# Queries and probabilities moved through DRAM with one write each, and the query split pinned behind the key copies, in a two-layer attention encoder

## The chip, the cores and the metric

The kernel runs on one core of a Trainium2 chip. The metric is the device time of one execution in microseconds. The median of three runs before the change is 906.31 us (905.59 to 910.03).

## The reference, cut to what matters

```python
D_MODEL = 1024; SEQ = 512; DEPTH = 2; HEAD_DIM = 64; N_HEADS = 16
DILATED_PAIRS = ((128, 1), (512, 4), (2048, 16))

def reference(x, norm_gain, a_w_in, a_w_out, ..., b_rpb):
    for i in range(DEPTH):
        hn = rms_norm(x, norm_gain[i])
        y = mixer_a(hn, ...) if i % 2 == 0 else mixer_b(hn, ...)
        x = x + y

def mixer_a(hn, w_in, w_out, q_gain, k_gain, t5_bias):
    proj = hn @ w_in                   # 3 groups of q, k, v, and one gate
    for g, (window, dilation) in enumerate(DILATED_PAIRS):
        q = rms_norm(qkv[:, :, g, 0], q_gain[g]); k = rms_norm(qkv[:, :, g, 1], k_gain[g])
        o, lse = dilated_group_attention(q, k, v, t5_bias[...], dilation, reach)
    alpha = softmax(stack(lses)); y = sum(alpha * stack(outs))
    return (y * silu(gate)) @ w_out
```

The first layer is a dilated sliding-window attention in three dilation groups, merged by their softmax denominators. The second (`mixer_b`) is a neighbourhood attention on an 8 x 64 grid with one group of q, k, v and a gate. All is float32.

## The kernel before, in words

Heads are worked in eight pairs (`hc` = 0 to 7, 128 columns each). A float32 product is made of three matmuls of split operands (`mm3`: high x high, high x low, low x high). Weights come in loads of 128 x 1024 (`wraw`, three buffers, L175), are split on ScalarE (`wh`, L127) and on VectorE or GpSimd (`wl`, L131), and are used by TensorE as `acc` matmuls, 128x512 each.

Two generators are run side by side. `main` emits the projections of a pair: keys and values of groups 1 and 2 (`rawk`), the queries and the keys of group 0 (`rawq`), the values of group 0 (`vt`), the gate (`gt`). `side` emits the attention of the pair before. `run` weaves them by a clock that counts matmul time, and `later_on(delay, job)` puts a job into the order at a due time of that clock, in ns. TensorE's order is the order written; on the other engines a scheduler of the framework places instructions by its own model, except those given to `tc.keep_in_program_order`. All transfers but two small ones are issued by SyncE (SP) in one queue. A transfer's issue also waits for the completion of the one eight places ahead of it, since eight completion counters are used in turn.

For one pair of the first layer the steps around the change are these.

- The projected keys and values are copied from PSUM to `rawk` on ScalarE (L458, eight copies of 128x256). GpSimd squares the keys (L272), VectorE reduces them, GpSimd computes the scale factors `rs` (L108 to L120), VectorE scales the keys (L295).
- `turn_q` transposes the scaled queries in 32x32 blocks on VectorE, in place in `rawq`. For pairs 0 to 5 (`moved`) `move_q` then sends them with sixteen SBUF-to-SBUF transfers of 64 KB into `qt` (L578), which completes the transposition.
- `split_q` makes the split operands of the group-0 scores: `k0h` (ScalarE, L598), `q0h` (ScalarE, L617 in `put_k`), `k0l` and `q0l` (VectorE, L601, L619). It is emitted after the key projection of the next pair, and is not pinned.
- The weighted sum of the earlier pair (`o` matmuls) is multiplied into its gate (`gt`, L668), which frees its PSUM bank. The scores (`log` matmuls) take four banks of the same pool of four, in two halves, u = 0 and 1.
- VectorE adds the bias and finds the extreme (`p`, L786, L797), ScalarE does the exponential (L808) and scaling (L648), VectorE transposes blocks into `tr` (L720). `turner.send` writes `tr` to DRAM (`td`, L729) in four writes of 256 KB, and reads it back into `pt` in four reads (L733), each into 32 partitions.
- The bias tiles `e` are loaded by six transfers for each pair (L683, L688).

In the second layer the probabilities of pairs 0 to 5 are moved by the same `turner.send`, with 224 KB for each write and read.

Of the kernel before, what the change touches and what calls it, by code (L numbers as in the profile page):

```python
# [13 lines left out]
F32 = mybir.dt.float32  # L14
F32R = mybir.dt.float32r
I32 = mybir.dt.int32
AF = mybir.ActivationFunctionType
# [5 lines left out]
P = 128  # L23
# [19 lines left out]
def tile_hybrid_encoder(  # L43
# [13 lines left out]
    nc = tc.nc  # L57
# [8 lines left out]
    dr = ctx.enter_context(tc.tile_pool(name="dr", bufs=1, space=DRAM))  # L66
# [132 lines left out]
    stamp = {(key, -1): 0 for key in ("k12", "q", "v", "qk")}  # L199
# [26 lines left out]
    def later_on(delay, job):  # L226

        timers.append((clock[0] + delay, job))
        timers.sort(key=lambda t: t[0])
# [132 lines left out]
    gk = cp.tile([P, 4], F32, name="gk")  # L362
# [55 lines left out]
    pq = wk.tile([P, 4096], F32, tag="pt", name="pt", bufs=1)  # L418
# [51 lines left out]
    def normed(raw, ss, ns, key, hc):  # L470
        head_norm(raw, ss, ns, key == "raw")
        if key == "rawq" and moved(hc):
            turn_q(raw)
        st[key, hc] = raw
        stamp[key, hc] = clock[0]
# [53 lines left out]

    def turn_q(raw):  # L530

        for a in range(0, 16, 4):
            v = raw[:, a : a + 4].rearrange("p f i r -> p (f i) r")
            nc.vector.transpose(v, v)

    def q_tiles():


        return (
            wk.tile([P, 512], F32R, tag="q0h", name="q0h", bufs=1),  # L540
            wk.tile([P, 512], F32R, tag="q0l", name="q0l", bufs=1),
            wk.tile([P, 4, 4, P], F32, tag="q12", name="qt", bufs=1),
            wk.tile([P, EXT], F32R, tag="k0h", name="k0h", bufs=1),
            wk.tile([P, EXT], F32R, tag="k0l", name="k0l", bufs=1),
        )
# [22 lines left out]

    def move_q(hc, raw):

        tiles = q_tiles()
        qt, left = tiles[2], [4]

        def move(a):
            for t in range(4):
                src = raw[32 * t : 32 * t + 32, 4 * a : 4 * a + 4].rearrange("k f i r -> k (f i r)")
                dst = qt[32 * a : 32 * a + 32, t].rearrange("k f x -> k (f x)")
                tc.keep_in_program_order(nc.sync.dma_start(dst, src))  # L578
            left[0] -= 1
            if a == 3:  # L580
                stamp["q", hc] = 0

        for a in range(4):
            later_on(1400 * a, partial(move, a))

        def land():
            yield "wait", ("rawk", hc + 1), 0
            assert not left[0]
            split_q(*tiles)
            st["q", hc] = tiles  # L590
            yield

        st["land", hc] = land()

    def split_q(q0h, q0l, qt, k0h, k0l):
        src = qt[:, :, 3, :].rearrange("p t (j r) -> p t r j", j=4)
        trj4 = lambda t: t[:, 64:EXT].rearrange("p (t r j) -> p t r j", t=4, j=4)
        nc.scalar.copy(trj4(k0h), src)  # L598
        by_t = lambda t: t.rearrange("p (t x) -> p t x", t=4)
        put_k([(by_t(q0h), by_t(q0l), qt[:, :, 0, :])], 0)  # L600
        nc.vector.tensor_sub(trj4(k0l), src, trj4(k0h.bitcast(F32)))  # L601

    def v_a(hc):

        yield "wait", ("vt", hc), 2500
        vt = st.pop(("vt", hc))
        tp = bank("tp")
        for i in range(4):
            transpose(tp[:, i * P : (i + 1) * P], vt[:, i * P : (i + 1) * P])
        nc.scalar.copy(v0[hc % 2], tp.rearrange("p (i c) -> p i c", i=4))  # L610
        stamp["v", hc] = 0
        yield

    def put_k(parts, g):

        for dh, _, src in parts:
            nc.scalar.activation(dh, src, AF.Copy, scale=gk[:, g : g + 1])  # L617
        for dh, dl, src in parts:
            nc.vector.scalar_tensor_tensor(  # L619
                dl, src, gk[:, g : g + 1], dh.bitcast(F32), op0=ALU.mult, op1=ALU.subtract  # L620
            )
# [87 lines left out]
    class turner:  # L709
# [12 lines left out]
        def send(self, dst, wait, pace):  # L722

            run = self.run
            d = dr.tile([4, P, run], F32, tag="td", name="td", bufs=2)
            place = dst.rearrange("p (a x) -> p a x", a=4)

            def write(b):
                tc.keep_in_program_order(nc.sync.dma_start(d[b], self.t[:, b * run : b * run + run]))  # L729

            def read(b):
                src = d[b].rearrange("(a k) x -> k a x", a=4)
                tc.keep_in_program_order(nc.sync.dma_start(place[32 * b : 32 * b + 32], src))  # L733
                self.left -= 1

            for b in range(4):
                later_on(pace * b, partial(write, b))
                later_on(wait + pace * b, partial(read, b))

    def attn_a(hc):  # L740
        e0, e12 = st.pop(("e", hc))
        q0h, q0l, qt, k0h, k0l = st.pop(("q", hc))
# [5 lines left out]
        def scores(u):  # L748

            tiles = []  # L750
            for t in (2 * u, 2 * u + 1):
                cs, n = (64, 192) if t == 0 else (0, 192) if t == 3 else (0, 256)
                tiles.append((t, [bank("log") for _ in range(2)], cs, n))
            for t, lgs, cs, n in tiles:
                ks = slice(P * t + cs, P * t + cs + n)
                qs = slice(P * t, P * t + P)
                mm3_heads(
                    [lg[:, cs : cs + n] for lg in lgs],
                    lambda hs: q0h[hs, qs], lambda hs: q0l[hs, qs],
                    lambda hs: k0h[hs, ks], lambda hs: k0l[hs, ks], False,  # L760
                )
            for t, lgs, cs, n in tiles:
                for g in range(2):
                    for j in range(4):
                        for hd in range(2):
                            hs = slice(64 * hd, 64 * hd + 64)
                            matmul(
                                lgs[hd][32 * j : 32 * j + 32, 256 + P * g : 384 + P * g],
                                qt[hs, t, 1 + g, 32 * j : 32 * j + 32],
                                k12[hs, g, P * j : P * j + P],  # L770
                                share=2,
                                start=False,
                                stop=(g == 1),
                            )
            return [
                (hd, t, softmax(hd, t, lgs[hd], cs, n)) for t, lgs, cs, n in tiles for hd in range(2)
            ]
# [34 lines left out]
        def turn_p(hd, t, pr):  # L812
            tp = bank("tp")
            for i in range(4):
                transpose(tp[:, i * P : (i + 1) * P], pr[:, i * P : (i + 1) * P])
            dst = sb(pts[0], at(t, 0, hd, 0), [[32, 4], [512, 4], [1, 32]])
            nc.vector.tensor_copy(dst, tp.rearrange("p (i a r) -> p i a r", i=4, a=4))
# [25 lines left out]
        if hc < NHC - 1:  # L843
            for u in range(2):
                if moved(hc):
                    if pending and u == 0:
                        pending.pop(0)()
                        yield
                    yield "wait", ("rawk", hc + 1), 4800 if u == 0 else 18500
                else:  # L850
                    yield 1200 if u == 0 else 8500
                turned = turner(512)
                turners.append(turned)
                for hd, t, pr in scores(u):
                    turned.put(pr, 512, 256 * hd + 128 * (t % 2))
                send = partial(turned.send, pq[:, 2048 * u : 2048 * u + 2048], 10500 - 1000 * u, 1200)
                later_on(7000 + 2000 * u, send)
                if pending and u == 0:
                    yield 5000
                    pending.pop(0)()  # L860
            pending.append(lambda: put_y(hc, weigh(), True, False))
        else:
            for u in range(2):
                if u == 0:
                    yield "wait", ("gate", hc), 500
                yield 600
                held = scores(u)
                yield 3200
                if pending:
                    yield "wait", ("gate", hc - 1), 16800  # L870
                    pending.pop(0)()
                    yield
                for args in held:
                    turn_p(*args)
                    yield
            yield from v_a(hc)
            stamp["ya", "turned"] = 0
            put_y(hc, weigh(), True, True)
            yield
# [392 lines left out]
```

## Time and profile before

| | |
|---|---|
| median of 3 runs | 906.31 us (905.59 to 910.03) |
| profiled execution, its own time | 905.46 us |
| its span | 903.7 us |
| TensorE busy, matmuls | 856.8 us (95%), 5547 |
| VectorE, ScalarE, GpSimd busy | 524.4, 427.6, 305.6 us |
| DMA | 134.97 MB, mean 149 GB/s |
| mean granted TensorE clock | 0.979 |

How to read the rows that follow. A row of the order of time gives the start and duration in us, the engine (PE is TensorE, DVE VectorE, ACT ScalarE, POOL GpSimd, SPq the queue of transfers on SyncE), the line of the kernel, the operation, output and inputs, a count, and in brackets the idle time before it with what ended it. A row of waits gives who waited for whom, the total in us, the number of times, and the longest. A row of the chain gives start, duration and what. A row of windows gives the stretch, its length, the busy time of TensorE's matmuls and weight loads, VectorE, ScalarE and GpSimd with counts, then the granted clock, the DMA engines' busy share and GB/s.

### The profile page before, as it was taken

What the parts mean: (1) busy time and instruction counts of PE and PEld (TensorE: products, weight loads), DVE (VectorE), ACT (ScalarE), POOL (GpSimd) and SP (SyncE); (2) the same over time, 40 slices, a digit from 0 to 9 for tenths busy, and PEclk for the clock granted to TensorE, in tenths of its full rate; (3) what the DMA queues carried; (4) which work ended last, traced back from release to release, by engine and by line L of the source; (5) the groups of instructions that cost most, each with busy time, mean ns of one, the idle gap of its engine ahead of it and who ended that gap; (6) DMA issues with size and microseconds to landing.
All of it is one profiled execution on the core that took longest, in us unless ns stands there. A gap on an engine that the chain in (4) does not pass through costs nothing.

```text
span 903.7 us, 15576 instructions
## 1 busy us (share of the span) xinstructions
PE 856.8 (95%) x5547; PEld 708.5 (78%) x5547; DVE 524.4 (58%) x1335; ACT 427.6 (47%) x924; POOL 305.6 (34%) x493
## 2 busy tenths in 40 slices
PE   8999999898799699699789999999999999999998
PEld 6788877687588488578668878778999888899776
DVE  6354594483576268258267675546566667666743
ACT  6434554452552363345255355445465556665541
POOL 2342532351442324234144134111433454434411
PEclk9999999999899899799989999999999999999999
DMA  6354287357257437634726847236326555656233
GB/s 235 105 147 128 91 244 188 108 143 209 84 162 211 126 109 204 162 118 114 215 78 170 235 130 198 66 121 219 99 87 180 161 150 150 165 157 178 101 102 126
DMA packets 64318, 134.97 MB, mean 149 GB/s; under 512 B 7920, under 2 KB 25264, under 8 KB 64240
## 3 DMA queue, kind: packets, MB, share of 16 engines
q1 hardware_dynamic: 63952, 133.96, 51.6%
q8 instruction: 44, 0.72, 0.3%
q14 instruction: 34, 0.28, 0.1%
q10 hardware_dynamic: 288, 0.01, 0.0%
HBM read 102.82 MB, written 24.83 MB: 141 GB/s over the span
## 4 chain that ended last, share of the span: by engine, by line
PE 67%; DMA 17%; DVE 5%; ACT 4%; SPq 4%; issue 2%; POOL 1%; ACTq 0%; DVEq 0%; POOLq 0%
PE acc L206 55%; DMA wraw<-in_w 7%; DMA td<-tr 5%; PE log L206 5%; PE o L206 4%; DMA e<-l_d 3%; SPq L578 2%; PE tp L210 2%; DMA qt<-rawq 1%; DVE wl L131 1%; DVE p L797 1%; ACT p L808 1%; ACT rawk L458 1%; ACT wh L127 1%; DMA pt<-td 1%
## 5 line engine op out<-in xcount | busy, mean ns | idle before, releaser
L206 PE MATMUL acc<-wh,hn_h 128*128 128x512 f32 (+1 forms) x768 | 299.0, 389 | 36.5 <-ACT rawk L458 34.6
L127 ACT CAST wh<-wraw 128x512 fp32r<-128x512 f32 (+1 forms) x276 | 161.1, 588 | 319.0 <-PE acc L206 217.2
L206 PE MATMUL acc<-wl,hn_h 128*128 128x512 f32 (+1 forms) x768 | 289.5, 377 | 0.4 <-DVE wl L131 0.4
L206 PE MATMUL acc<-wh,hn_l 128*128 128x512 f32 (+1 forms) x768 | 289.7, 377 | 0.0
L131 POOL TENSOR_TENSOR wl<-wraw,wh 128x512 fp32r<-128x512 f32 (+1 forms) x110 | 140.5, 1277 | 407.3 <-ACT wh L127 372.6
L206 PEld LDWEIGHTS acc<-wh,hn_h 128*128 128x128 f32 x768 | 146.8, 191 | 67.8 <-ACT rawk L458 37.1
L131 DVE TENSOR_TENSOR wl<-wraw,wh 128x512 fp32r<-128x512 f32 (+1 forms) x166 | 121.6, 733 | 134.5 <-ACT wh L127 129.7
L206 PEld LDWEIGHTS acc<-wh,hn_l 128*128 128x128 f32 x768 | 146.6, 191 | 21.6
L206 PEld LDWEIGHTS acc<-wl,hn_h 128*128 128x128 f32 x768 | 147.1, 192 | 20.1 <-DVE wl L131 0.9
L206 PE MATMUL acc<-hn_h,wh 128*128 128x512 f32 x192 | 77.8, 405 | 1.0 <-ACT rawq L458 0.8
L206 PE MATMUL acc<-hn_l,wh 128*128 128x512 f32 x192 | 75.0, 391 | 0.0
L206 PE MATMUL acc<-hn_h,wl 128*128 128x512 f32 x192 | 75.0, 391 | 0.0
L272 POOL TENSOR_TENSOR sq<-rawk 128x256 f32<-128x256 f32 x64 | 42.5, 676 | 87.2 <-ACT rawk L458 80.5
L648 ACT ACTIVATE p<-p,mn 128x512 f32<-128x512 f32 (+3 forms) x128 | 68.6, 586 | 0.0
L808 ACT ACTIVATE p<-p,mn 128x512 f32<-128x512 f32 (+1 forms) x64 | 44.9, 702 | 48.7 <-DVE mn L797 48.7
L720 DVE STREAM_TRANSPOSE tr<-p 128x512 f32<-128x512 f32 (+1 forms) x80 | 53.6, 683 | 9.4 <-ACT p L648 9.0
L273 DVE TENSOR_REDUCE ss<-sq 128x4 f32<-128x256 f32 (+1 forms) x96 | 48.1, 502 | 18.5 <-POOL sq L272 15.1
L206 PE MATMUL acc<-y_h,wh 128*128 128x512 f32 x128 | 52.1, 407 | 0.0
L206 PE MATMUL acc<-y_h,wl 128*128 128x512 f32 x128 | 50.0, 391 | 0.0
L206 PE MATMUL acc<-y_l,wh 128*128 128x512 f32 x128 | 50.0, 390 | 0.0
L206 PEld LDWEIGHTS acc<-hn_h,wh 128*128 128x128 f32 x192 | 36.1, 188 | 12.7 <-ACT rawq L458 2.9
L206 PEld LDWEIGHTS acc<-hn_h,wl 128*128 128x128 f32 x192 | 36.0, 188 | 7.9
(138 smaller groups left out, 1072.3 us busy)
## 6 DMA issues: line engine op xcount, KB each, us to landing
wraw<-in_w SPq DMA_DIRECT2D x95, 512.0 KB
wraw<-in_w SPq DMA_DIRECT2D x38, 384.0 KB
td<-tr SPq DMA_DIRECT2D x56, 256.0 KB
pt<-td SPq DMA_DIRECT2D x56, 256.0 KB
qt<-rawq SPq DMA_DIRECT2D x96, 64.0 KB
td<-tr SPq DMA_DIRECT2D x24, 224.0 KB
pt<-td SPq DMA_DIRECT2D x24, 224.0 KB
e<-l_d SPq DMA_DIRECT2D x32, 112.0 KB
```

Source lines behind the costliest of these rows:

```text
L127: nc.scalar.copy(h, raw)
L131: eng.tensor_sub(l, raw, h.bitcast(F32))
L206: nc.tensor.matmul(o, l, r, **kw)
L210: nc.tensor.transpose(o, i, ident)
L272: nc.gpsimd.tensor_mul(sq, v, v)
L273: nc.vector.tensor_reduce(ss[:, i * ns : (i + 1) * ns], sq.rearrange("p (a b) -> p a b", b=64), axis=AX.X, op=ALU.add)
L458: nc.scalar.activation(dst, src, AF.Copy, scale=rs_n[:, i : i + 1])
L578: tc.keep_in_program_order(nc.sync.dma_start(dst, src))
L648: nc.scalar.activation(pr, pr, AF.Copy, scale=mn[:, 3:4])
L720: nc.vector.transpose(dst, src[:, :n].rearrange("p (i b k) -> p i b k", b=4, k=32))
L797: nc.vector.tensor_tensor_reduce(out=v(pr), in0=v(lg), in1=e12[:, 2 * hd : 2 * hd + 2, 96 - 32 * t : 224 - 32 * t], scale=1.0, scalar=mn[: ...
L808: nc.scalar.activation(row, row, AF.Exp, bias=mn[:, 1:2], scale=-1.0, accum_out=mn[:, 2:3])
```

## The change

The queries go to a DRAM tile with one write of 1 MB and come back in four reads of 256 KB, in the order 0, 2, 1, 3. The write is due 600 ns after the start of `move_q`, the reads 5500 ns after it. The probabilities are written in one transfer too; their reads stay four, in the same changed order. The two copies of the query split on ScalarE are kept in program order, behind the key copies of the next pair. `turn_q` runs its four transposes over the token blocks. Three due times of the scores and of the sends are moved: 4800 to 5200, 18500 to 17800, and the wait of the reads from 10500 and 9500 to 8500.

```diff
     def turn_q(raw):
-        for a in range(0, 16, 4):
-            v = raw[:, a : a + 4].rearrange("p f i r -> p (f i) r")
-            nc.vector.transpose(v, v)
+        for i in range(4):
+            nc.vector.transpose(raw[:, :, i, :], raw[:, :, i, :])
...
     def move_q(hc, raw):
+        d = dr.tile([4, P, 512], F32, name="qd", tag="qd", bufs=2)
         tiles = q_tiles()
         qt, left = tiles[2], [4]
-        def move(a):
-            for t in range(4):
-                src = raw[32 * t : 32 * t + 32, 4 * a : 4 * a + 4].rearrange("k f i r -> k (f i r)")
-                dst = qt[32 * a : 32 * a + 32, t].rearrange("k f x -> k (f x)")
-                tc.keep_in_program_order(nc.sync.dma_start(dst, src))
+        def write():
+            src = raw.rearrange("p (a f) i r -> p a (f i r)", f=4)
+            tc.keep_in_program_order(nc.sync.dma_start(d.rearrange("a p x -> p a x"), src))
+            stamp["q", hc] = 0
+        def read(a):
+            dst = qt[32 * a : 32 * a + 32].rearrange("k t f x -> k t (f x)")
+            src = d[a].rearrange("(t k) x -> k t x", t=4)
+            tc.keep_in_program_order(nc.sync.dma_start(dst, src))
             left[0] -= 1
-            if a == 3:
-                stamp["q", hc] = 0
-        for a in range(4):
-            later_on(1400 * a, partial(move, a))
+        later_on(600, write)
+        for a in (0, 2, 1, 3):
+            later_on(5500, partial(read, a))
...
     def split_q(q0h, q0l, qt, k0h, k0l):
-        nc.scalar.copy(trj4(k0h), src)
+        tc.keep_in_program_order(nc.scalar.copy(trj4(k0h), src))
-        put_k([(by_t(q0h), by_t(q0l), qt[:, :, 0, :])], 0)
+        put_k([(by_t(q0h), by_t(q0l), qt[:, :, 0, :])], 0, True)
...
-    def put_k(parts, g):
+    def put_k(parts, g, pinned=False):
         for dh, _, src in parts:
-            nc.scalar.activation(dh, src, AF.Copy, scale=gk[:, g : g + 1])
+            m = nc.scalar.activation(dh, src, AF.Copy, scale=gk[:, g : g + 1])
+            if pinned:
+                tc.keep_in_program_order(m)
...
     class turner: def send(self, dst, wait, pace):
-            def write(b):
-                tc.keep_in_program_order(nc.sync.dma_start(d[b], self.t[:, b * run : b * run + run]))
+            src = self.t[:, : 4 * run].rearrange("p (b x) -> p b x", b=4)
+            tc.keep_in_program_order(nc.sync.dma_start(d.rearrange("b p x -> p b x"), src))
-            for b in range(4):
-                later_on(pace * b, partial(write, b))
-                later_on(wait + pace * b, partial(read, b))
+            for n, b in enumerate((0, 2, 1, 3)):
+                later_on(wait + pace * n, partial(read, b))
...
     def attn_a(hc):
-                    yield "wait", ("rawk", hc + 1), 4800 if u == 0 else 18500
+                    yield "wait", ("rawk", hc + 1), 5200 if u == 0 else 17800
-                send = partial(turned.send, pq[:, 2048 * u : 2048 * u + 2048], 10500 - 1000 * u, 1200)
+                send = partial(turned.send, pq[:, 2048 * u : 2048 * u + 2048], 8500, 1200)
```

## The prediction

> **What bounds the kernel now.** I read the page first, then who waited for whom on TensorE, then TensorE's order of time for its longer gaps.
>
> ```profile
> span 903.7 us, 15576 instructions
> PE 856.8 (95%) x5547; PEld 708.5 (78%) x5547; DVE 524.4 (58%) x1335; ACT 427.6 (47%) x924; POOL 305.6 (34%) x493
> ```
> ```profile
> PE acc L206 <- ACT rawk L458: 34.6, 5, 8.5
> PE log L206 <- DVE gt L668: 2.4, 1, 2.4
> ...
> PE acc L206 <- DVE wl L131: 0.4, 1, 0.4
> ```
> ```profile
> 154.34 0.50 PE L206 MATMUL acc<-wh,hn_h 128*128 128x512 f32 x1 [1.74 <-ACT rawk L458]
> ...
> 165.03 0.38 PE L206 MATMUL log<-k0h,q0h 64*128 64x256 f32 x1 [2.40 <-DVE gt L668]
> ...
> 231.74 0.79 PE L206 MATMUL acc<-wh,hn_h 128*128 128x512 f32 x1 [8.37 <-ACT rawk L458]
> ...
> 305.97 0.79 PE L206 MATMUL acc<-wh,hn_h 128*128 128x512 f32 x1 [7.96 <-ACT rawk L458]
> ...
> 380.31 0.80 PE L206 MATMUL acc<-wh,hn_h 128*128 128x512 f32 x1 [7.95 <-ACT rawk L458]
> ...
> 455.77 0.79 PE L206 MATMUL acc<-wh,hn_h 128*128 128x512 f32 x1 [8.55 <-ACT rawk L458]
> ```
>
> TensorE is busy for 856.8 of 903.7 us, so nearly all that can be won without removing matmuls is its 46.9 us of idle time. Most of it is six gaps, all in the first layer: four of about 8 us, one for each of head pairs 2 to 5, and two small ones around pair 1. In the large ones TensorE has finished the next pair's keys and wants their accumulators back; ScalarE has not copied them out (L458). ScalarE's and SyncE's orders of time, and the chain that ended last, tell why:
>
> ```profile
> 303.50 1.06 ACT L598 CAST k0h<-qt 128x512 fp32r<-128x512 f32 x1 [6.47 <-DMA qt<-rawq]
> ...
> 305.10 3.01 ACT L458 ACTIVATE rawk<-acc,rs_n 128x256 f32<-128x256 f32 x8
> ```
> ```profile
> 268.38 0.34 SPq L729 DMA_DIRECT2D td<-tr  x1
> 279.68 0.30 SPq L733 DMA_DIRECT2D pt<-td  x1
> ...
> 288.16 13.75 SPq L578 DMA_DIRECT2D qt<-rawq  x16
> ```
> ```profile
> 231.74 3.66 PE acc L206 x9
> ...
> 240.62 1.99 PE log L206 x75
> ...
> 301.32 2.01 DMA qt<-rawq
> ...
> 305.97 4.05 PE acc L206 x9
> ...
> 317.23 11.80 PE acc L206 x51
> ...
> 380.31 4.21 PE acc L206 x9
> ...
> 455.77 4.21 PE acc L206 x9
> ```
>
> The split of the queries (k0h, L598) stands ahead of the eight key copies on ScalarE and sat 6.47 us waiting for the moved queries. Their sixteen small DMAs took 13.75 us to issue. So a late transfer held work that does not need it. After each gap the clock is low as well: nine matmuls took 3.66 to 4.21 us, where 51 in a row took 11.80, or 0.231 each and 2.08 for nine.
>
> **Part by part. (1) The pin.** In the compiled order of the changed kernel all six pairs have the eight key copies, then one weight cast, then the query split. The four large waits go: 8.37 + 7.96 + 7.95 + 8.55 = 32.8 us. Their slow restarts go too: 3.66 + 4.05 + 4.21 + 4.21 = 16.1 less 4 x 2.08, which is 7.8. Pair 1 offers its two gaps and the half clock after the second:
>
> ```profile
> 154.40:156.60 2.20, 2.20 (x9) 1.40 (x9) 1.83 (x4) 2.20 (x7) 2.05 (x4) 1.00 0.00 0
> 165.10:169.70 4.60, 4.60 (x76) 3.50 (x77) 3.36 (x19) 3.29 (x7) 1.53 (x1) 0.64 0.00 0
> ```
>
> These are windows; the third column from the right is the granted clock. The gap of 1.74 us left it at 1.00, the one of 2.40 was followed by 0.64 for 4.6 us, a loss of 4.6 x 0.36 = 1.7. Pair 1 has 1.74 + 2.40 + 1.7 = 5.8. All that can go is 32.8 + 7.8 + 5.8 = 46.4 us, or 9.3 for each of five pairs.
>
> **(2) What is late next: VectorE.** In the changed order VectorE does the key scaling (L295) ahead of the product that frees the output's PSUM bank (gt, L668). Before, only pair 1 had that order, and its 2.40 us gap is the price. The rows:
>
> ```profile
> 161.88 2.50 DVE L295 TENSOR_TENSOR rawk<-rawk,rs 128x256 f32<-128x256 f32 x4 [3.95 <-POOL rs L120]
> 164.30 0.67 DVE L668 TENSOR_TENSOR gt<-gt,o 128x512 f32<-128x512 f32 x1
> ```
> ```profile
> 313.31 0.22 POOL L120 TENSOR_TENSOR rs<-rs,na 128x16 f32<-128x16 f32 x1
> ```
> ```profile
> 314.30 1.42 DVE L295 TENSOR_TENSOR rawk<-rawk,rs 128x256 f32<-128x256 f32 x4
> ```
> ```profile
> 162.33 0.30 PE L206 MATMUL log<-k0h,q0h 64*128 64x256 f32 x1
> ```
>
> Let K be the moment TensorE has finished a pair's keys. GpSimd's scale factors were ready 313.53 - 308.11 = 5.4 us after the last copy (305.10 + 3.01). Copies that wait for nothing end a quarter of 3.01 us after K, at K + 0.8, so the factors come at K + 6.2. Scaling is 1.42 or 2.50 and the product 0.67: the bank is free at K + 8.3 to K + 9.4. TensorE wants it 162.33 - 154.34 + 0.2 = 8.2 us after it goes on from K. That leaves a wait of 0.1 to 1.2 us in each of pairs 1 to 5. I take 1.2, the row in which GpSimd works beside VectorE as it will here. Between 1.74 (no half clock) and 2.40 (half clock) lies the threshold; small delays can push 1.2 over it, so I add half of 1.7: 2.0 us a pair, 10 us in all, between 0.5 and 14.5.
>
> The Trainium skill, "TensorE: Matmul & The Clock Gate", section "What's actually happening", puts the fall to half rate after an idle window of about 3.4 us. By that the waits would cost 1.2 a pair, 6 in all, and the time would be 4 us lower. The trace is harsher: a 2.40 us gap was followed by half rate.
>
> **(3) The queries through DRAM.** Nothing in the trace shows this round trip, so it is built from windows. (last column GB/s)
>
> ```profile
> 281.00:293.00 12.00, 12.00 (x56) 9.91 (x56) 3.51 (x7) 4.05 (x8) 2.59 (x2) 1.00 1.01 290
> 296.00:302.00 6.00, 2.02 (x9) 1.32 (x8) 0.69 (x1) 0.62 (x1) 0.00 (x0) 1.00 0.39 90
> 342.00:347.00 5.00, 5.00 (x23) 4.13 (x22) 4.65 (x8) 1.00 (x2) 3.73 (x4) 1.00 1.06 230
> ```
>
> The first is a full queue (290 GB/s), the second the small query copies alone (90), the third mostly the four reads of probabilities (230). Count from the scores' start S = 240.62; K was 305.97 - 7.96 = 298.0, S + 57.4. The second write of probabilities landed by 279.68, S + 39.1; being four times as large it takes about 2 us more, S + 41. In the new order four reads (1 MiB), three weights (1.5 MiB) and the query write (1 MiB) follow: 3.67 MB at 290 GB/s is 12.7 us, S + 54. The four query reads wait at the head of SyncE's queue for that landing; behind them stand three weight loads. They need 1.05 MB at 230 GB/s, 4.6, and 2.0 from issue to landing as the last small copy did (301.32): S + 60.4, K + 3.0. The splits:
>
> ```profile
> 304.60 1.05 DVE L601 TENSOR_TENSOR k0l<-qt,k0h 128x512 fp32r<-128x512 f32 x1 [6.84 <-ACT k0h L598]
> 305.57 0.74 DVE L619 SCALAR_TENSOR_TENSOR q0l<-qt,gk,q0h 128x512 fp32r<-128x512 f32 x1
> ```
>
> 1.06 + 1.05 + 0.74 end at K + 5.9, just ahead of the scale factors (K + 6.2). So the queries cost nothing, but with 0.3 us in hand: each microsecond later is one on TensorE in each pair. With the reads at 290 GB/s they land at K + 2.0, at 90 (11.7 us) at K + 10. I take 230, a read into 32 partitions like these.
>
> **(4) Fewer, larger DMAs.** A pair issues 15 transfers for queries and probabilities in place of 32, which takes the 13.75 us stretch from SyncE's queue. A megabyte more passes per pair (3.6 us at 290 GB/s); a pair's period is 305.97 - 231.74 = 74.2 us and stays at 64 or more, so the engines have room. The queue standing for landings is nothing new: it stood 279.68 - 268.38 = 11.3 us, and TensorE waited 0.4 us in all for split weights.
>
> **(5) The rest at nothing.** The four query transposes take other strides:
>
> ```profile
> L720 DVE STREAM_TRANSPOSE tr<-p x80: 529/706/714, 107.1 to 815.5; 128x512 f32<-128x512 f32 x68, 128x384 f32<-128x384 f32 x12
> ```
> ```profile
> 650.00:904.00 254.00, 248.63 (x1526) 217.60 (x1524) 152.26 (x442) 132.18 (x347) 95.20 (x182) 1.00 0.48 140
> ```
>
> The nearest strided form takes 0.71 us each, on an engine that is not late there. The moved due times shift scores by under a microsecond and take nothing off TensorE. In the second layer the same single write replaces four; TensorE is busy 248.6 of 254 us there and the probabilities are wanted a pair later, which hides it. Without that cover it would cost the write's 3.6 us in each of six pairs, 22 us.
>
> **The sum.** The profiled execution took 905.46 us, 0.85 under the median of 906.31. 905.46 - 46.4 + 10 = 869.1; on the median's scale 870.
>
> **The rivals.** *Queries late.* For it: only 0.3 us in hand, and a round trip that needs two landings in a row. Against it: fewer issues bring the write forward. Queries at K + 6 to K + 10 need 2.85 + 1.42 + 0.67 = 4.9 more and so make waits of 2.7 to 6.7 us; with 1.7 of half clock that is 4.4 to 8.4 a pair, 22 to 42 us in place of 10. The time is 882 to 902.
>
> *Slower: the query write is caught in the queue.* If the write takes the 11.3 us that the small write took behind the bias loads, not its 3.6 share, and the reads go at 90 GB/s, the queries land 7.7 + 7.1 later, at K + 17.8. Then splits 2.85, scaling 1.42 and product 0.67 give K + 22.7, a wait of 14.5 and 2 of slow clock: 82 us over five pairs, 942 us. It decides from queries at about K + 11, where the loss passes 9.3 a pair. Against it: the bias loads stand ahead of the second write of probabilities, and the query write only follows that one's landing.
>
> *The change does not do what it says.* If the copies still waited as before, 906. The compiled order speaks against it.
>
> **How the numbers follow.** The forecast has 0.73 (860 to 880), late queries 0.17 (882 to 902), the slower case 0.06, no effect 0.04. The range starts at 860, where all 46.4 us go and nothing comes back, and reaches to 895, well into the late case; some 0.15 is left out above. A difference under 0.5%, 4.5 us, is about what a measurement of this kernel can't tell from none. Late queries reach that band only at their upper end, so: faster 0.89, same 0.04, slower 0.07.
>
> **What would show it.** Right: no TensorE wait on the key copies over 1 us; a wait on that product of 0.5 to 2.5 us in pairs 1 to 5; the query split waiting under 2 us for its DMA; the period of a pair near 66 us in place of 74.2. Wrong: score matmuls waiting on q0l or k0l for 4 us or more, weight casts waiting on loads until TensorE stops, or the second layer growing.

## The result and the profile after

The changed kernel takes 880.14 us in the median of four runs (878.36 to 881.69), the one before 908.17 us (905.59 to 913.37) beside it. The ratio is 0.9684, with a 95% interval of 0.9633 to 0.9735: faster by 28 us, where 36 were forecast. The time lies inside the forecast range of 860 to 895, 10 us above the 870 that was forecast and at the upper edge of the 860 to 880 that had the largest chance. The profiled execution took 881.69 us. Here and below the ratios are formed from runs in the faster of two states of the chip and the medians from all runs, which differ by one run: 878.36 us, in the experiment with the old transfers and the right order.

The page of the changed kernel, and who waited for whom on TensorE (total us, times, longest):

```profile
span 879.9 us, 15373 instructions
PE 855.7 (97%) x5547; PEld 711.0 (81%) x5547; DVE 522.9 (59%) x1335; ACT 430.6 (49%) x924; POOL 304.9 (35%) x493
```
```profile
PE log L206 <- DVE gt L673: 13.6, 5, 2.8
PE acc L206 <- ACT rawq L458: 2.1, 2, 1.4
```

TensorE does the same 5547 matmuls in almost the same busy time; its idle time fell from 46.9 to 24.2 us. The row `PE acc <- ACT rawk`, 34.6 us before, is gone. The row `PE log <- DVE gt` has grown from one wait to five. TensorE's order of time shows where they lie, one in each of pairs 1 to 5:

```profile
163.19 0.58 PE L206 MATMUL log<-k0h,q0h 64*128 64x256 f32 x1 [2.83 <-DVE gt L673]
...
233.38 0.38 PE L206 MATMUL log<-k0h,q0h 64*128 64x256 f32 x1 [2.76 <-DVE gt L673]
...
302.06 0.47 PE L206 MATMUL log<-k0h,q0h 64*128 64x256 f32 x1 [2.67 <-DVE gt L673]
...
370.66 0.58 PE L206 MATMUL log<-k0h,q0h 64*128 64x256 f32 x1 [2.67 <-DVE gt L673]
...
440.76 0.38 PE L206 MATMUL log<-k0h,q0h 64*128 64x256 f32 x1 [2.65 <-DVE gt L673]
```

The windows of 7 us behind each of the five (the third column from the right is the granted clock, the share of its full clock that TensorE had):

```profile
163.20:170.20 7.00, 7.00 (x81) 5.57 (x82) 4.12 (x21) 4.85 (x11) 1.53 (x1) 0.58 0.00 0
233.40:240.40 7.00, 7.00 (x86) 5.63 (x87) 4.34 (x22) 5.24 (x12) 1.54 (x1) 0.76 0.02 4
302.10:309.10 7.00, 7.00 (x86) 5.70 (x87) 4.12 (x21) 4.96 (x12) 1.54 (x1) 0.76 0.00 0
370.70:377.70 7.00, 7.00 (x80) 5.54 (x81) 4.12 (x21) 4.85 (x11) 1.53 (x1) 0.53 0.01 2
440.80:447.80 7.00, 7.00 (x86) 5.49 (x87) 4.79 (x23) 5.70 (x13) 1.56 (x1) 0.76 0.01 2
```

Each wait was followed by a slow stretch. The shares lost add up to 0.42 + 0.24 + 0.24 + 0.47 + 0.24 = 1.61 of 7 us, 11.3 us. So one wait of about 8 us for each of four pairs became one of about 2.7 us for each of five, and the clock fell after every one. In all that is 13.6 + 11.3 = 24.9 us that the better order did not win.

One pair and the second layer, as windows:

```profile
302.10:370.70 68.60, 65.93 (x454) 53.44 (x454) 42.16 (x100) 31.95 (x63) 24.23 (x36) 0.97 0.60 180
626.00:879.90 253.90, 249.18 (x1532) 218.04 (x1530) 151.00 (x443) 132.13 (x347) 96.15 (x183) 1.00 0.46 140
```

A pair takes 68.6 us in place of 74.2. The last 254 us hold almost the same work as before (1532 matmuls against 1526), and from the sums of the second layer's norm (tile `pk`) to the end it is 260.9 us in place of 261.3: the second layer is as long as it was.

### The profile page after: what moved, and what is told of

The parts are those of the page before. It is cut to its first block, busy times and chain, and to the rows that moved or that the text cites. A ratio compares the mean times of both kernels' runs of the same rounds, so it can differ in the third digit from the quotient of the medians.

```text
span 879.9 us, 15373 instructions
## 1 busy us (share of the span) xinstructions
PE 855.7 (97%) x5547; PEld 711.0 (81%) x5547; DVE 522.9 (59%) x1335; ACT 430.6 (49%) x924; POOL 304.9 (35%) x493
## 4 chain that ended last, share of the span: by engine, by line
PE 84%; DVE 5%; ACT 4%; POOL 3%; DMA 2%; issue 1%; SPq 0%; ACTq 0%; POOLq 0%; DVEq 0%
PE acc L206 72%; PE log L206 5%; PE tp L210 3%; PE o L206 3%; ACT rawk L458 2%; DVE rawk L295 1%; DMA qd<-rawq 1%; ACT p L1065 1%; POOL na L118 1%; ACT p L653 1%; POOL na L113 1%; DMA qt<-qd 1%; DMA hg<-in_head_gain 1%; POOL na L119 0%; POOL rs L120 0%
## 5 line engine op out<-in xcount | busy, mean ns | idle before, releaser
L131 POOL TENSOR_TENSOR wl<-wraw,wh 128x512 fp32r<-128x512 f32 (+1 forms) x110 | 136.8, 1243 | 367.4 <-ACT wh L127 337.3
L131 DVE TENSOR_TENSOR wl<-wraw,wh 128x512 fp32r<-128x512 f32 (+1 forms) x166 | 114.9, 693 | 156.3 <-ACT wh L127 151.9
L272 POOL TENSOR_TENSOR sq<-rawk 128x256 f32<-128x256 f32 x64 | 40.5, 638 | 52.1 <-ACT rawk L458 44.2
L295 DVE TENSOR_TENSOR rawk<-rawk,rs 128x256 f32<-128x256 f32 x64 | 34.0, 591 | 22.7 <-POOL rs L120 22.3
```

What stands on the lines that cost most here:

```text
L131: eng.tensor_sub(l, raw, h.bitcast(F32))
L272: nc.gpsimd.tensor_mul(sq, v, v)
L295: m = nc.vector.tensor_mul(v, v, by)
```

## The experiments

Six kernels were run, one of them twice: the first four on one chip beside runs of the kernel before (median 909.54 us, 903.50 to 914.10), the other three on another (908.08, 906.22 to 915.53). Theory and rival are those of each expectation. They ask what the pin and the transfers are worth apart, and whether the wait on the product kept the rest of the forecast gain.

**The pin alone.** The kernel before, with the split's two ScalarE copies pinned (`put_k` pins its copy when it is given True) and all transfers as they were.

```diff
-        nc.scalar.copy(trj4(k0h), src)
+        tc.keep_in_program_order(nc.scalar.copy(trj4(k0h), src))
-        put_k([(by_t(q0h), by_t(q0l), qt[:, :, 0, :])], 0)
+        put_k([(by_t(q0h), by_t(q0l), qt[:, :, 0, :])], 0, True)
```

> The kernel before with the pin alone: the two copies of the query split stay behind the key copies, the sixteen small transfers of queries and all else stay as they were. Theory A (the pin carries the gain, the transfers through DRAM little): the queries of before landed 5.3 us after the keys' last matmul (303.35 against 298.0), so the split ends at 8.2, key scaling and the product follow, and TensorE waits some 3.5 us on the product instead of 2.7: about 5 us over the changed kernel, 880 to 888 us. Rival B (both parts are needed): in a shorter pair the small transfers land later against the keys, by up to 4 us more, each of which is a microsecond on TensorE: 895 to 905 us, with TensorE or VectorE waiting on k0h and its DMA.

Measured: 890.74 us (884.08 to 894.13), ratio 0.978 (0.9713 to 0.9848). TensorE's waits, and ScalarE's order of time around the key copies of pair 3:

```profile
PE log L206 <- DVE gt L670: 13.1, 5, 2.7
PE acc L206 <- ACT rawk L458: 3.8, 3, 1.6
```
```profile
294.31 0.62 ACT L127 CAST wh<-wraw 128x512 fp32r<-128x512 f32 x1 [3.27 <-DMA wraw<-in_w]
294.83 3.02 ACT L458 ACTIVATE rawk<-acc,rs_n 128x256 f32<-128x256 f32 x8
...
302.12 1.14 ACT L598 CAST k0h<-qt 128x512 fp32r<-128x512 f32 x1 [3.76 <-DMA qt<-rawq]
```

The time fell between the ranges of the two theories, so neither number was right. The pin takes away most of the key-copy waits (3.8 us left of 34.6) and brings in a wait on the product of the size that the whole change has (13.1 against 13.6 us). In pair 3 the chain behind it is another, though: the late queries hold the split, the split ends at 305.0 us on VectorE, and scaling and product follow at once. And the old transfers still cost something: a weight cast ahead of the key copies sat 3.27 us waiting for its load, the copies came late behind it (TensorE stood 1.62 us for them), and the split sat 3.76 us waiting for its queries. ScalarE's waits for weight loads total 90.5 us here (89.5 in the kernel before) and 31.5 us with the whole change.

**The transfers alone.** The changed kernel without the pin.

```diff
-        tc.keep_in_program_order(nc.scalar.copy(trj4(k0h), src))
+        nc.scalar.copy(trj4(k0h), src)
-        put_k([(by_t(q0h), by_t(q0l), qt[:, :, 0, :])], 0, True)
+        put_k([(by_t(q0h), by_t(q0l), qt[:, :, 0, :])], 0)
```

> The changed kernel without the pin: its transfers and due times, but the query split free to go ahead of the key copies on ScalarE, as the scheduler then puts it. Theory A: the key copies wait for the queries again, which land 0.6 to 3.2 us after the keys' last matmul; TensorE waits 3 to 6 us on the key copies of pairs 2 to 5, but not on the product, which the scheduler then puts ahead of key scaling: 882 to 897 us. Rival B (the transfers carry most of the gain): queries land so early that the copies hardly wait: 865 to 880 us. If the transfers gave nothing at all: 905.

Measured: 895.80 us (892.61 to 898.66), ratio 0.9859 (0.9806 to 0.9913). The first row is TensorE's wait, the others ScalarE's order of time in pair 3:

```profile
PE acc L206 <- ACT rawk L458: 27.5, 5, 8.1
```
```profile
302.74 1.06 ACT L601 CAST k0h<-qt 128x512 fp32r<-128x512 f32 x1 [6.62 <-DMA qt<-qd]
...
304.85 3.01 ACT L458 ACTIVATE rawk<-acc,rs_n 128x256 f32<-128x256 f32 x8
```

The split stands ahead of the key copies again and holds them, 27.5 us in all. So the new path by itself does not bring the queries early enough for that order. The time is in Theory A's range; of the waits of pairs 2 to 5 three lie in its 3 to 6 us and one, 8.1 us, above. There is no wait on the product here: without the pin the scheduler puts the product ahead of the scaling. Pin alone 19 us, transfers alone 14, both 28: the two parts overlap.

**The product first.** The changed kernel, with the scaling of the keys held back until the product of the earlier pair has been emitted (pairs 1 to 5; in pair 0, whose scaling is held too, there is no earlier product), and scaling and product kept in program order.

```diff
-        head_norm(raw, ss, ns, key == "raw")
+        head_norm(raw, ss, ns, key == "raw" or (key == "rawk" and 1 <= hc < NHC - 1))
...
-            nc.vector.tensor_mul(gt, gt, o)
+            tc.keep_in_program_order(nc.vector.tensor_mul(gt, gt, o))
...
                         pending.pop(0)()
+                    while later and u == 0:
+                        later.pop()()
+                    if u == 0:
                         yield
```

> The changed kernel with the product that frees the output's PSUM bank ahead of the key scaling on VectorE (product and scaling kept in program order, product first). If the five waits of 2.7 us and the half clock behind them come from that order: 13.6 + 9.9 us go, about 857 us, and the rows of a score matmul waiting on the product vanish or fall under 0.5 us. Rival: the scores then wait as long for the low parts of the split queries (k0l, q0l), which end 5 us after the keys, or for something else: 870 us or more.

Measured: 859.18 us (856.74 to 861.09), ratio 0.9456 (0.9406 to 0.9505). VectorE's order of time in pair 3, and the longest that is left of TensorE's waits:

```profile
287.26 0.69 DVE L673 TENSOR_TENSOR gt<-gt,o 128x512 f32<-128x512 f32 x1 [1.39 <-PE o L206]
288.96 3.86 DVE L295 TENSOR_TENSOR rawk<-rawk,rs 128x256 f32<-128x256 f32 x4 [1.01 <-POOL rs L120]
```
```profile
PE acc L206 <- ACT rawq L458: 4.4, 3, 2.2
```

The product now waits only for its own matmuls (`o`), the scaling follows, and no score waits for it. That one swap on VectorE brings 21 us (880.14 to 859.18; the intervals of the two ratios lie apart), most of the 24.9 counted above. It shows that the wait on the product and its slow stretches were what kept the change from its forecast.

**Scale factors on VectorE.** The changed kernel with the scale factors of the keys moved from GpSimd.

```diff
-    def head_norm(raw, ss, ns, held):
+    def head_norm(raw, ss, ns, held, key=None):
...
-        rsqrt(nc.vector if ns == 8 else nc.gpsimd, rs[:, : 4 * ns], ss[:, : 4 * ns], 4 * ns, 1.0 / DH)
+        rsqrt(nc.vector if ns == 8 or len(raw.shape) == 3 and key == "rawk" else nc.gpsimd, ...)
...
-        head_norm(raw, ss, ns, key == "raw")
+        head_norm(raw, ss, ns, key == "raw", key)
```

> The changed kernel with the scale factors of the keys (L108 to L120, group rawk) computed on VectorE in place of GpSimd; the scheduler may order VectorE anew. If what holds the product is GpSimd's chain (7.5 us after the keys' last matmul, slowed by a microsecond beside the query split on VectorE): the wait falls under 0.5 us a pair, 857 to 864 us. Rival: VectorE's eleven small operations, its scaling and the split in a row are as late: 875 to 885 us.

Measured: 864.62 us (862.83 to 870.15), ratio 0.9527 (0.9472 to 0.9583). The time ends 0.6 us past the range of the theory, far from the rival's. But the run does not isolate GpSimd, as was meant: the scheduler put the product ahead of the scaling here too, in all five pairs. The one long wait on the product that is left, 2.40 us, came about in another way. VectorE's, ScalarE's and TensorE's orders of time:

```profile
288.91 1.08 DVE L604 TENSOR_TENSOR k0l<-qt,k0h 128x512 fp32r<-128x512 f32 x1 [2.48 <-ACT k0h L601]
...
293.50 0.68 DVE L673 TENSOR_TENSOR gt<-gt,o 128x512 f32<-128x512 f32 x1
294.09 1.43 DVE L295 TENSOR_TENSOR rawk<-rawk,rs 128x256 f32<-128x256 f32 x4
```
```profile
287.79 1.09 ACT L601 CAST k0h<-qt 128x512 fp32r<-128x512 f32 x1 [2.31 <-DMA qt<-qd]
```
```profile
294.23 0.58 PE L206 MATMUL log<-k0h,q0h 64*128 64x256 f32 x1 [2.40 <-DVE gt L673]
```

In this pair the split waited 2.31 us for its queries, `k0l` waited for the split, and the product stood behind `k0l`, `q0l` and ten small steps of the factors. That is the rival of late queries, in one pair.

**The old transfers, with the right order.** The pin and the product first, but the sixteen small query copies and the four writes of the kernel before. The edit is the pin's and the product's above, on the kernel before, so the old due times and transposes stay as well.

> The kernel before with the pin and with the product ahead of the key scaling, but its sixteen small query transfers and four probability writes as they were. Theory A (the transfers through DRAM matter only by when the queries land): against the kernel with the pin alone the five waits on the product go, 13.1 us, and some 8 of half clock, which leaves waits on the split queries of up to 3 us a pair: 868 to 880 us, 10 to 20 over the kernel with the changed transfers and the product first. Rival B (once the order on ScalarE and VectorE is right the transfers are hidden): 856 to 863 us, the same as with them.

Measured: 873.10 us (864.52 to 878.36), ratio 0.9587 (0.9522 to 0.9651). The same order with the new transfers, beside it on the same chip, is the last experiment: 860.63 us, ratio 0.9473 (0.9447 to 0.9499). By the ratios the new path, with its due times and strides, is worth some 10 us once no score waits for the product; the intervals lie apart by little. That is Theory A's time, but not its reason: TensorE's waits on the low parts of the split queries total 0.6 us in the profiled execution. That execution is the fastest of the four, 864.52 us, and shows only part of the loss:

```profile
ACT wh L127 <- DMA wraw<-in_w: 68.5, 22, 7.6
...
ACT k0h L598 <- DMA qt<-rawq: 11.8, 4, 3.5
```

These are ScalarE's waits; in the last experiment the two totals are 37.7 and 2.0 us. How much of them reaches TensorE is not shown, and where the slower runs of this kernel lose up to 14 us more was not traced.

**Four writes of the probabilities.** The product-first kernel, but the probabilities go out in four writes with their old due times.

```diff
-            src = self.t[:, : 4 * run].rearrange("p (b x) -> p b x", b=4)
-            tc.keep_in_program_order(nc.sync.dma_start(d.rearrange("b p x -> p b x"), src))
+            def write(b):
+                tc.keep_in_program_order(nc.sync.dma_start(d[b], self.t[:, b * run : b * run + run]))
...
             for n, b in enumerate((0, 2, 1, 3)):
+                later_on(pace * n, partial(write, b))
                 later_on(wait + pace * n, partial(read, b))
...
-                send = partial(turned.send, pq[:, 2048 * u : 2048 * u + 2048], 8500, 1200)
+                send = partial(turned.send, pq[:, 2048 * u : 2048 * u + 2048], 10500 - 1000 * u, 1200)
```

> The changed kernel with the product first, but the probabilities written in four writes with the due times they had before; the queries stay with one write and four reads. Theory A (the query path is the part of the transfers that counts): within 4 us of the kernel with the product first, 855 to 863 us. Rival B (SyncE's queue is freed by the single write of probabilities, and the queries depend on that): the queries land later by 3 to 6 us and the time is 870 us or more.

Measured: 861.28 us (859.03 to 863.67), ratio 0.9488 (0.9461 to 0.9515), against 0.9473 (0.9447 to 0.9499) for the product-first kernel beside it. The single write of the probabilities is worth nothing that these runs can tell.

**The product first, again,** on the second chip, unchanged.

> The changed kernel with the product first once more, beside the two others on the same chip: 857 to 861 us.

Measured: 860.63 us (858.52 to 861.52), ratio 0.9473 (0.9447 to 0.9499). The gain holds: 20 us under the changed kernel and 47 under the one before. No version is faster; the one with four writes is level with it.

## Why the prediction was right, and where its size was off

**The pin, step 1: right.** It forecast that all key-copy waits and their slow restarts go; with pair 1's two gaps and the slow stretch behind them that made 46.4 us. No such wait is left, and SyncE's and ScalarE's rows show why:

```profile
277.02 0.43 SPq L576 DMA_DIRECT2D qd<-rawq  x1
...
285.58 1.74 SPq L582 DMA_DIRECT2D qt<-qd  x4
```
```profile
289.50 3.03 ACT L458 ACTIVATE rawk<-acc,rs_n 128x256 f32<-128x256 f32 x8
292.37 0.67 ACT L127 CAST wh<-wraw 128x512 fp32r<-128x512 f32 x1
292.88 1.18 ACT L601 CAST k0h<-qt 128x512 fp32r<-128x512 f32 x1
```

The key copies wait for nothing, one weight cast follows, and the split then starts without idling.

**The late product, step 2: the right place, the wrong size.** The term was 2.0 us a pair, 10 in all. It measured 24.9 over five pairs, 5.0 each: the term of the sum that failed. The working for pair 3 can be laid beside it. K, the end of the keys, is where the first of the nine `acc` matmuls ahead of the `o` matmuls starts, 291.34. TensorE wanted the bank 2.67 us before 302.06, at 299.39: 8.05 us after K, where the forecast had 8.2. GpSimd's order of time in that pair, and VectorE's:

```profile
294.34 0.87 POOL L113 TENSOR_TENSOR na<-rs 128x16 f32<-128x16 f32 x1
295.29 0.64 POOL L118 TENSOR_TENSOR na<-na,nv 128x16 f32<-128x16 f32 x1
...
296.60 0.21 POOL L113 TENSOR_TENSOR na<-rs 128x16 f32<-128x16 f32 x1
296.89 0.22 POOL L118 TENSOR_TENSOR na<-na,nv 128x16 f32<-128x16 f32 x1
...
298.68 0.22 POOL L120 TENSOR_TENSOR rs<-rs,na 128x16 f32<-128x16 f32 x1
```
```profile
294.09 1.09 DVE L604 TENSOR_TENSOR k0l<-qt,k0h 128x512 fp32r<-128x512 f32 x1 [0.18 <-ACT k0h L601]
295.09 0.75 DVE L624 SCALAR_TENSOR_TENSOR q0l<-qt,gk,q0h 128x512 fp32r<-128x512 f32 x1
298.93 2.48 DVE L295 TENSOR_TENSOR rawk<-rawk,rs 128x256 f32<-128x256 f32 x4 [3.09 <-POOL rs L120]
301.33 0.67 DVE L673 TENSOR_TENSOR gt<-gt,o 128x512 f32<-128x512 f32 x1
```

- The copies ended at 292.53, K + 1.2; forecast K + 0.8.
- The factors were ready at 298.90, 6.4 us after the copies, not 5.4. The 5.4 came from a pair of the kernel before where the split had already run. In the new order the split runs beside GpSimd's chain, and two small steps took 0.87 and 0.64 us where the same steps took 0.21 and 0.22 once VectorE was done: 1.1 us. The forecast had laid the split and the factors side by side, ending at K + 5.9 and K + 6.2, without a price for it.
- The scaling took 2.48; the forecast had taken 2.50, the longer of its two rows. The product ended at 302.00, K + 10.7 in place of K + 9.4.

So 1.2 us of wait became 2.7. Pair 1 of the kernel before, the one row with this order, had waited 2.40 us; the forecast put a chain of parts in its place that made half of that. (The row was not quite the same case: there the copies ended 2.1 us after TensorE went on.) And the slow stretch, which the forecast counted in half of the pairs at 1.7 us, came in all of them, at 1.7 to 3.3 us. The sum with the measured terms is 905.46 - 46.4 + 24.9 = 884.0; the execution took 881.69. The 2.3 us between are not placed. Had the wait and its slow stretches been as small as forecast, the same sum would give near 870; with none at all 860 was measured, the low end of the range. Of the signs named in advance two were missed by little: the wait on the product (2.65 to 2.83 us against 0.5 to 2.5) and the period of a pair (68.6 against 66). That the range still held is in part luck: it had been stretched past 880 for late queries, which did not come, and the 15 us by which step 2 was too small fitted into that room.

**The queries through DRAM, step 3: right in outcome, and a little earlier than forecast.** The chain that ended last gives both legs:

```profile
277.02 8.50 DMA qd<-rawq
...
286.89 5.08 DMA qt<-qd
```

The write took 8.5 us, over twice the 3.6 that the forecast gave it as its share, but it was issued early enough to land at 285.52, K - 5.8, where the forecast had S + 54, K - 3.4. From there to the landing of the reads it took 6.4 us, forecast 6.6. So the reads landed at 291.97, K + 0.6; the forecast had K + 3.0. In pair 2 there was nothing to spare:

```profile
225.81 1.09 ACT L601 CAST k0h<-qt 128x512 fp32r<-128x512 f32 x1 [1.54 <-DMA qt<-qd]
```

No score waited on the split operands. The slower rival, a write caught in the queue until the queries are late, did not happen, though 8.5 us is nearer to its 11.3 than to 3.6; late queries appeared only as the 1.54 us here and 0.42 us in pair 1.

**Fewer, larger DMAs, step 4: under-rated.** The forecast gave it no time beside the pin. The pin alone ended at ratio 0.978, the whole change at 0.9684. These come from two sets of runs and their intervals overlap a little; with the product first the two paths differ on one chip by some 10 us, with intervals that lie apart. It is the query path, with its due times and strides, that pays and not the single write of the probabilities. ScalarE's waits for weight loads and for queries are shorter with it, but that these bring the 10 us is not shown.

**The rest, step 5: right.** The second layer is as long as it was. The 24 query transposes took 16.1 us of VectorE's time in place of 14.9, and no row of TensorE's waits names them; no run took the strides or the due times apart from the rest.

## What to carry to other kernels

When a held-up engine is released, follow what is queued behind its work on every engine and ask which wait ends last in the new order. A duration or a chain length taken from the old order is only good if the same work runs beside it in the new one. Here putting one product ahead of a scaling of 2.5 us brought 21 us, three quarters of what the whole change did, because that scaling stood in TensorE's way five times and each time the clock fell as well.

## What the runs showed of the hardware

The forecast looked for a threshold between 1.74 and 2.40 us of idle time past which the clock falls. There is none as sharp as that. In the last experiment, the second run of the product-first kernel, two almost equal gaps, of 2.09 and 2.10 us, ended differently, and in the pin-alone kernel a gap of 2.67 us left the clock alone. TensorE's order of time, then the windows, first of the one kernel and then of the other:

```profile
185.08 0.50 PE L206 MATMUL acc<-hn_h,wh 128*128 128x512 f32 x1 [2.09 <-ACT rawq L458]
...
200.39 0.50 PE L206 MATMUL acc<-wh,hn_h 128*128 128x512 f32 x1 [2.10 <-ACT gt L492]
```
```profile
185.10:192.10 7.00, 7.00 (x31) 5.80 (x32) 5.96 (x9) 3.41 (x6) 6.43 (x6) 1.00 0.48 124
200.40:207.40 7.00, 7.00 (x24) 5.60 (x25) 5.33 (x8) 1.78 (x3) 1.56 (x2) 0.76 0.64 176
```
```profile
161.96 0.38 PE L206 MATMUL log<-k0h,q0h 64*128 64x256 f32 x1 [2.67 <-DVE gt L670]
```
```profile
162.00:169.00 7.00, 7.00 (x93) 5.72 (x94) 4.80 (x23) 5.68 (x13) 1.57 (x1) 1.00 0.00 0
```

In the nine traces ten gaps of 1.36 to 1.74 us left the clock at 1.00, and of the 16 gaps of 2.09 to 2.83 us 13 were followed by a slow stretch. In the stretch behind 370.70 in the changed kernel, cut into slices of 0.6 us, the granted clock is 0.50, half rate. Counted at half rate, a stretch lasted 3.4 us in seven cases (0.24 of 7 us lost) and 5.2 to 6.6 us in six. The length of the gap does not decide which: of the two gaps of 2.67 us in the changed kernel one has 0.76 behind it and one 0.53. The Trainium skill, "TensorE: Matmul & The Clock Gate", section "What's actually happening", has the gate watch a window of about 3.4 us that runs on by itself, whatever the kernel does. A stretch of 3.4 us, and two equal gaps with unequal ends, agree with such a window; that a whole idle window is needed does not, since 2.10 us were enough here.

GpSimd's steps of 0.21 and 0.22 us took 0.87 and 0.64 us while VectorE ran the split, and each ended within 0.1 us of the VectorE instruction beside it (295.21 and 295.93 against 295.18 and 295.84). The Trainium skill, "GPSIMD Engine Reference", section "1. Specifications", says that the two share their way to the on-chip memory when VectorE reads two inputs from there, as these two instructions do; the rows agree, though no run here separated the sharing from other causes.
